# Cache moves due earlier, and the a/b projection as fp32 products on four column groups

## The chip, the cores and the metric

The kernel runs on one core of one Trainium2 chip, in one launch. The metric is the device time of one execution in microseconds (us), as the median of a few runs. Lower is better.

## The reference, cut to what matters

One decoder step is computed for a prompt of 512 tokens and for 8 samples of 4 tokens each (32 tokens), 544 tokens in all, width 1024. Everything is fp32.

```python
shift, scale, gate = jnp.split(jax.nn.silu(c) @ w_cond + b_cond, 3, axis=-1)
h = x * (1 + scale[:, None]) + shift[:, None]
qa, ka, va, za, qkv_b, zb, a_b, b_b, g_a, g_b = split_columns(h @ w_in)   # 11280 columns
# branch A: sliding-window attention, three groups of heads; the samples' keys are
#           cache rows (128, 512 and 2048 of them) followed by their four new rows
# branch B: gated delta rule; its decay comes from a_b and its beta from b_b (8 columns each)
merged = sigmoid(g_a) * (yA @ w_branch_a) + sigmoid(g_b) * (yB @ w_branch_b)
x = LayerNorm(ALPHA * x + gate * (merged @ w_out)) * ln_g + ln_b
# also returned: the samples' caches moved up by four rows, with the new rows at the end
kv_new.append(ext[:, ext.shape[1] - n_buf:])
```

Two pieces of this matter below. The 16 columns a and b of the projection are a small product (1024 by 16) for all 544 tokens. The returned caches are, but for the four new rows, a copy of 84 MB from one place in HBM to another, on which no computation waits.

## The kernel before

**How it is built.** The function `body` doesn't issue instructions. It records them (class `Recorder`), and `Recorder.schedule` then puts them in order with a list scheduler: it keeps its own estimate of when each engine and each operand is free, and takes on each engine the ready operation of lowest rank, then of lowest number. An operation may carry a due time `at`, ahead of which it isn't taken. `emit` then issues everything in that order on five in-order queues (PE, DVE, ACT, POOL, SP); since it is one line of code, all instructions in the profile carry the line L735, and they are told apart by their tiles' names.

**The front.** The scale comes from `cond_block(1, c, m, ...)`, which multiplies silu(c) (`cs`) by a piece `wc` of the conditioning weights: eight fp32 products into four column groups of one bank (`tile_position=(0, 32 * q)`), then `Y`, then products with `sel`, which add the four groups up. Each chunk of `sc` makes `x1`, the scaled x as two parts `x1h` and `x1l` (high part and remainder in float32r). The first three tiles of the projection are built from `x1` while the scale still arrives. Behind them stands the product for a and b: the weight columns 384 to 399 of `W3` are split into high and low part in one tile of 32 columns, `hl`, and for each half of the tokens (272 columns) 16 products `pg<-x1h,hl` and `pg<-x1l,hl` add up in one bank; ACT copies both halves to `abT`. The shift is put on later (`W3` by `sh`, then additions on `ab`), and `gates()` makes the decays from `abT` with products against `sel16` and `selab`, which add the high and low rows.

**The stream.** The rest of the projection, the two branch products and the gates run as a stream of jobs (`stream`): a job's weights are loaded into `wt` (three buffers, 512 KB each), split by ACT into `hi` and by DVE into `lo`, and multiplied with `hhi` and `hlo` (the two parts of h) in 48 products of 272 columns into `pp`. The stream has rank 9, so attention (`pg`), delta rule (`pd`, `pb`) and everything else go ahead of it when they are ready, and it fills the rest. The samples' attention comes in two halves: the first (`slab` tiles) runs beside the prompt's attention, the second (`kv` tiles, 32 loads of 512 KB of keys and values) from about 660 us on, after the samples' delta rule (`S0` tiles).

**The cache moves.** 168 moves of 128 rows each copy the caches from `cache{g}` to `kv{g}_s`, all issued on SP. They have rank 30, the last of all, and are spread evenly by their due times between two numbers:

```python
MOVES = (48.0, 850.0)
    d.at = MOVES[0] + (MOVES[1] - MOVES[0]) * i / len(moves)
```

The scheduler also holds a rank-30 move back while more than four of its eight tracked transfers are in flight. Weight loads, the samples' keys and values, and many small round trips through HBM use the same SP queue.

Of the kernel before, what the change touches and what calls it, by code (L numbers as in the profile page):

```python
# [11 lines left out]
F32 = mybir.dt.float32  # L12
F32R = mybir.dt.float32r
AF = mybir.ActivationFunctionType
# [6 lines left out]
KT = 8  # L21
SEQ = 512
# [3 lines left out]
NT = SEQ + NS  # L26
HF = NT // 2
# [8 lines left out]
BIG = 1e30  # L36
BANKS = (2, 2, 3, 1)
MOVE = 128
MOVES = (48.0, 850.0)
GATES = (110.0, 200.0)  # L40
EARLY_A, EARLY_B = 7, 4
S0B = 7
# [208 lines left out]
class Recorder:  # L251
# [22 lines left out]
    def pool(self, make, name, bufs, side):  # L274
        return Pool(self, make, name, bufs, side)
# [512 lines left out]
def body(ctx, tc, io):  # L788
    rec = Recorder()
    pe, ve, se, ge, sp = rec.engines()  # L790
# [19 lines left out]
    def pg():  # L810
        return psg.tile([128, 512], F32, name="pg", tag="g")
# [4 lines left out]
    def pb_():  # L816
        return psb.tile([128, 512], F32, name="pb", tag="b")
# [14 lines left out]
    def C(name, where="early"):  # L832
        a, n = CCOLS[name]
        return tables[where][:, a:a + n]
# [13 lines left out]
    op = pool(octx, "opool", 9, "right")  # L848
# [41 lines left out]
    xT = fx.tile([128, KT, NT], F32, name="xT")  # L890
    W3 = fx.tile([128, KT, 400], F32, name="W3")
    sc = fx.tile([128, KT, 9], F32, name="sc")
    sh = fx.tile([128, KT, 32], F32, name="sh")
    early_ = op.tile([128, NT], F32, name="cg", tag="o")
    n = CONST[2].shape[1]
# [1 line left out]
    dta = early_[:, n:n + 68].rearrange("p (a b) -> p a b", b=34)  # L897
    shifts = early_[:, n + 68:n + 104].rearrange("p (a b) -> p a b", b=9)
    first = [op.tile([128, NT], F32, name="raw", tag="o") for _ in range(3)]
    abT = op.tile([128, NT], F32, name="abT", tag="o")[0:32]  # L900
    xs = xT[:, :, SEQ:].rearrange("p k (b t) -> p k b t", t=4)
    per_token = lambda t, k, n: t[:, k:k + n, 1:9, None].to_broadcast([128, n, 8, 4])
    cols_of = lambda n: slice(n * HF, (n + 1) * HF)
    with ExitStack() as fctx:
        fr = pool(fctx, "front", 1)
# [27 lines left out]
        sp.dma_start(bnw, io["b_norm_w"])  # L933
        ve.memset(cs, 0.0)
        ge.memset(sh, 0.0)
        th = fr.tile([128, KT, 9], F32, name="th")
        se.activation(th, cT, AF.Tanh, scale=0.5)
        ve.tensor_scalar(th, th, 0.5, 0.5, op0=OP.mult, op1=OP.add)
# [2 lines left out]
        def cond_block(part, at, m, other):  # L941

            ps, wc, w = pb_() if other else pg(), pieces[part, at], 128 * m
            idle = IDLE if (part, at) == (1, 0) else (0, 0, 0)
            rec.rank = -1

            def turn_over(n):
                for _ in range(n):
                    pe.matmul(ps[:, 384:512], ones, ones, start=True, stop=True)

            turn_over(idle[0])
            with rec.together():
                for k in range(KT):
                    q = k % 4
                    pe.matmul(ps[32 * q:32 * q + 32, 0:w].rearrange("p (a b) -> p a b", b=128), cs[:, k, :], wc[:, :, k, :],
                              start=(k < 4), stop=(k >= 4), tile_position=(0, 32 * q)).at = 9.9 * ((part, at) == (1, 1))
                turn_over(idle[1])
            Y = fr.tile([128, 256], F32, name="Y", bufs=2)
            ve.tensor_copy(Y[:, 0:w], ps[:, 0:w])
            pv = ps[:, 256:256 + 16 * m].rearrange("p (a b) -> p a b", b=16)  # L960
            with rec.together():
                for i in range(m):
                    pe.matmul(pv[:, i, 0:9], Y[:, 128 * i:128 * i + 128], C("selc", "first"), start=True, stop=True)
                turn_over(idle[2])
            rec.rank = 0
            return pv[:, :, 0:9], bT[:, 8 * part + at:8 * part + at + m, None].to_broadcast([128, m, 9])

        x1 = [fr.tile([128, KT, NT], F32R, name=f"x1{u}") for u in "hl"]
        sums = [[f()[:, :HF] for _ in range(2)] for f in (pp, pd, pg)]
        for b, (c, m) in enumerate(CHUNKS):  # L970
            pv, bias = cond_block(1, c, m, b % 2)
            kk = slice(c, c + m)
            ve.scalar_tensor_tensor(sc[:, kk], pv, 1.0, bias, op0=OP.add, op1=OP.add)
            for k in range(c, c + m):
                se.activation(x1[0][:, k, :SEQ], xT[:, k, :SEQ], AF.Copy, scale=sc[:, k, 0:1])
                if k == c:
                    ve.tensor_mul(xs[:, kk], xs[:, kk], per_token(sc, c, m))
                    se.activation(x1[0][:, kk, SEQ:], xT[:, kk, SEQ:], AF.Copy)
                    ve.tensor_sub(x1[1][:, kk, SEQ:], xT[:, kk, SEQ:], x1[0][:, kk, SEQ:].bitcast(F32))
                ve.scalar_tensor_tensor(x1[1][:, k, :SEQ], xT[:, k, :SEQ], sc[:, k, 0:1], x1[0][:, k, :SEQ].bitcast(F32),  # L980
                                        op0=OP.mult, op1=OP.subtract)
            hi, lo = (wsp.tile([128, D], F32R, name=n, tag=n)[:, 0:384 * m].rearrange("p (k c) -> p k c", k=m) for n in ("hi", "lo"))
            se.activation(hi, W3[:, kk, 0:384], AF.Copy)
            ve.tensor_sub(lo, W3[:, kk, 0:384], hi.bitcast(F32))
            for k in range(c, c + m):
                for t in range(3):
                    w, w_ = (x[:, k - c, 128 * t:128 * t + 128] for x in (hi, lo))
                    for n in range(2):
                        for a, x in ((w, 0), (w, 1), (w_, 0)):
                            pe.matmul(sums[t][n], a, x1[x][:, k, cols_of(n)], start=(k == 0 and a is w and x == 0),  # L990
                                      stop=(k == KT - 1 and a is w_))
        for t in range(3):
            for n in range(2):
                rec.either(first[t][:, cols_of(n)], sums[t][n])
        hl = fr.tile([128, KT, 32], F32R, name="hl")
        se.activation(hl[:, :, 0:16], W3[:, :, 384:400], AF.Copy)
        ve.tensor_sub(hl[:, :, 16:32], W3[:, :, 384:400], hl[:, :, 0:16].bitcast(F32))
        ps = [pg(), pg()]
        for n in range(2):
            for k in range(KT):  # L1000
                for x in range(2):
                    pe.matmul(ps[n][0:32, :HF], hl[:, k], x1[x][:, k, cols_of(n)],
                              start=(k == 0 and x == 0), stop=(k == KT - 1 and x == 1))
        for n in range(2):
            se.activation(abT[:, cols_of(n)], ps[n][0:32, :HF], AF.Copy)
        for c, m in two_by_two:
            pv, bias = cond_block(0, c, m, c % 4)
            kk = slice(c, c + m)
# [2 lines left out]
        ps, pv = pg(), pb_()  # L1011
        with rec.together():
            for k in range(KT):
                q = k % 4
                pe.matmul(ps[32 * q:32 * q + 32, 0:400], sh[:, k, :], W3[:, k, :], start=(k < 4), stop=(k >= 4),
                          tile_position=(0, 32 * q))
# [80 lines left out]
    for i, (g, b, r0, r1) in enumerate(moves):  # L1097
        d = mv.dma_start(io[f"kv{g}_s"][b, r0:r1], io[f"cache{g}"][b, r0 + 4:r1 + 4])
        d.at = MOVES[0] + (MOVES[1] - MOVES[0]) * i / len(moves)
    rec.rank = 0  # L1100
# [29 lines left out]
    def gates():  # L1130
# [14 lines left out]

        pa = pg()
        for c in range(4):
            pe.matmul(pa[:, c * 16:c * 16 + 16], abT[:, c * 128:(c + 1) * 128], C("sel16", "g")[0:32], start=True, stop=True)
        sab = C("selab", "g").rearrange("p (a b) -> p a b", b=4)
        for h4 in range(4):  # L1150
            pe.matmul(pa[32 * h4:32 * h4 + 32, 64:68], abT[:, SEQ:], sab[0:32, h4, :], start=True, stop=True)
        zero = op.tile([128, NT], F32, name="zero", tag="o")[0:16, 0:512]
        ge.memset(zero, 0.0)
        ab = d1.tile([128, 2, 34], F32, name="ab")
# [36 lines left out]
        g = d1.tile([128, 34], F32, name="g")  # L1191
# [355 lines left out]
    pairs = [{} for _ in range(4)]  # L1547
# [637 lines left out]
    rules = threads.add(chain(delta_rule), 0)  # L2185
    blocks = threads.add(chain(delta_blocks), 1)
    threads.add(gates(), -2)
    threads.add(stream(57 + 4 + EARLY_B), 9)
    ap = pool(actx, "ap", 1)
# [125 lines left out]
    for k in range(0, KT, 2):  # L2315
        name = ("hi", "lo")[k // 4]
# [69 lines left out]
    for tt, n in ((0, 0), (1, 0), (2, 0), (None, 0), (0, 1), (1, 1), (2, 1), (3, 0), (3, 1)):  # L2386
# [3 lines left out]
        q = r[tt]  # L2390
        step = 256 if n and tt == 3 else 512
        for c in range(512 * n, 512 * n + 512, step):
            po = product_out(tt, c, c + step)
            w = slice(c, c + step)
# [129 lines left out]
```

## Time and profile before

| | us |
|---|---|
| median of 3 runs | 878.49 |
| lowest and highest | 874.96, 881.58 |
| the profiled execution: its time | 876.41 |
| its span, first to last instruction | 874.6 |
| mean granted TensorE clock | 0.995 |

| engine | busy us | share of the span |
|---|---|---|
| PE (TensorE) | 860.4 | 98% |
| DVE (VectorE) | 644.2 | 74% |
| ACT (ScalarE) | 452.0 | 52% |
| POOL (GpSimd) | 66.1 | 8% |

[...] The DMA engines are busy for four fifths of the span, moving 236 MB.

### The profile page before, as it was taken

The page shows a single profiled execution, that of the slowest core. Times are in us where ns is not written, and L with a number is a line of the kernel's source. Part 1 is how long each engine was busy: PE and PEld are TensorE (multiplying, and loading weights), DVE is VectorE, ACT ScalarE, POOL GpSimd, SP SyncE. Part 2 cuts the span into 40 slices and gives each one's busy share as a digit, 9 for nine tenths or more (in the row PEclk, how much of TensorE's full clock was granted, in tenths as well). Part 3 has the DMA queues.
Part 4 walks back from the last instruction along what each step waited for, and adds up shares of the span by engine and source line. Part 5 has one row for each costly group of instructions (what it writes and reads, how often), then busy time and mean ns, then how long its engine had stood idle before and what let it go on. Part 6 is the DMA issues. An engine that isn't in the chain of part 4 may idle for free.

```text
span 874.6 us, 20691 instructions
## 1 busy us (share of the span) xinstructions
PE 860.4 (98%) x8152; PEld 812.8 (93%) x8152; DVE 644.2 (74%) x1326; ACT 452.0 (52%) x1071; POOL 66.1 (8%) x167
## 2 busy tenths in 40 slices
PE   8999999999999999999999999999999999999996
PEld 7889999898999999998999998999999999999875
DVE  4775557565447999866999963564999999968547
ACT  3546556765646776446776446733442213334442
POOL 0120110110001010001110000011010000001000
PEclk9999999999999999999999999999999999999998
DMA  9876768756596969979788887469869899989983
GB/s 338 344 217 189 240 216 261 252 203 222 182 265 222 314 213 270 297 218 340 248 270 272 273 254 257 161 215 337 335 186 360 320 354 369 384 284 331 363 289 138
DMA packets 120493, 236.18 MB, mean 270 GB/s; under 512 B 49110, under 2 KB 76576, under 8 KB 117708
## 3 DMA queue, kind: packets, MB, share of 16 engines
q1 hardware_dynamic: 120396, 234.86, 79.6%
q8 instruction: 64, 1.05, 0.5%
q14 instruction: 33, 0.27, 0.1%
HBM read 218.53 MB, written 103.97 MB: 369 GB/s over the span
## 4 chain that ended last, share of the span: by engine, by line
PE 92%; DVE 3%; ACT 2%; DMA 1%; issue 1%; SPq 1%; DVEq 0%
PE pp L735 69%; PE pg L735 10%; PE pd L735 9%; PE pb L735 4%; DMA wc<-in_w_cb 1%; ACT L735 1%; SPq L735 1%; DVE acc L735 0%; DVE lo L735 0%; ACT sq L735 0%; DMA out_kv_s<-in_cache 0%; DVE gt L735 0%; DVE r L735 0%; DVE slab L735 0%; DVE zt L735 0%
## 5 line engine op out<-in xcount | busy, mean ns | idle before, releaser
L735 PE MATMUL pp<-hhi,hi 128*128 128x272 f32 x1360 | 399.1, 293 | 0.5 <-DVE zt L735 0.5
L735 PE MATMUL pp<-hhi,lo 128*128 128x272 f32 x1360 | 397.1, 292 | 0.0
L735 PE MATMUL pp<-hlo,hi 128*128 128x272 f32 x1360 | 395.8, 291 | 0.0
L735 PEld LDWEIGHTS pp<-hhi,hi 128*128 128x128 f32 x1360 | 257.0, 189 | 3.3 <-issue 2.6
L735 PEld LDWEIGHTS pp<-hhi,lo 128*128 128x128 f32 x1360 | 257.0, 189 | 1.8 <-issue 1.1
L735 PEld LDWEIGHTS pp<-hlo,hi 128*128 128x128 f32 x1360 | 257.0, 189 | 1.5 <-issue 0.4
L735 ACT ACTIVATE hi<-wt 128x1024 fp32r<-128x1024 f32 (+1 forms) x101 | 103.4, 1024 | 159.4 <-PE pp L735 134.2
L735 DVE TENSOR_TENSOR lo<-wt,hi 128x1024 fp32r<-128x1024 f32 (+1 forms) x101 | 119.1, 1179 | 84.4 <-ACT hi L735 80.8
L735 DVE SCALAR_TENSOR_TENSOR acc<-ext,cw,acc 128x568 f32<-128x568 f32 x72 | 57.9, 804 | 2.1 <-ACT acc L735 1.1
L735 DVE TENSOR_REDUCE slab<-slab 128x8 f32<-128x512 f32 (+2 forms) x66 | 42.4, 660 | 2.6 <-ACT slab L735 2.5
L735 DVE TENSOR_TENSOR slab<-slab 128x512 f32<-128x512 f32 (+1 forms) x66 | 43.0, 670 | 0.4 <-DMA slab<-in_ks 0.3
L735 ACT ACTIVATE zt<-pp 128x272 f32<-128x272 f32 x48 | 18.7, 390 | 46.1 <-PE pp L735 45.9
L735 ACT ACT_TABLE_LOAD x32 | 41.1, 1283 | 2.4 <-PE pp L735 1.0
L735 PE MATMUL pp<-ybh,lo 128*128 128x272 f32 x128 | 37.1, 290 | 0.0
L735 PE MATMUL pp<-ybh,hi 128*128 128x272 f32 x128 | 36.9, 288 | 0.0
L735 PE MATMUL pp<-ybl,hi 128*128 128x272 f32 x128 | 36.9, 288 | 0.0
L735 ACT ACTIVATE P<-P,st 128x256 f32<-128x256 f32 (+1 forms) x64 | 31.1, 487 | 6.8 <-DVE st L735 6.6
L735 DVE CUSTOM_DVE_ANT_0 P<-pg,bias 128x256 f32<-128x256 f32 (+1 forms) x64 | 23.3, 404 | 12.9 <-PE pg L735 12.9
L735 POOL COPY cx<-ext 128x3 f32<-128x3 f32 (+1 forms) x48 | 22.2, 490 | 140.1 <-ACT ext L735 138.6
L735 ACT ACTIVATE spare<-pp 128x272 f32<-128x272 f32 (+1 forms) x32 | 16.2, 507 | 19.1 <-PE pp L735 19.1
L735 PEld LDWEIGHTS pp<-ybh,lo 128*128 128x128 f32 x128 | 24.2, 189 | 0.6 <-issue 0.4
L735 PEld LDWEIGHTS pp<-ybh,hi 128*128 128x128 f32 x128 | 24.2, 189 | 0.1
(419 smaller groups left out, 1539.0 us busy)
## 6 DMA issues: line engine op xcount, KB each, us to landing
out_kv_s<-in_cache SPq DMA_DIRECT2D x144, 512.0 KB
wt<-in_w_in SPq DMA_DIRECT2D x85, 512.0 KB
out_kv_s<-in_cache SPq DMA_DIRECT2D x24, 496.0 KB
wc<-in_w_cb SPq DMA_DIRECT2D x16, 512.0 KB
slab<-in_ks SPq DMA_DIRECT2D x32, 256.0 KB
slab<-in_vs SPq DMA_DIRECT2D x32, 256.0 KB
kv<-in_ks SPq DMA_DIRECT2D x16, 512.0 KB
kv<-in_vs SPq DMA_DIRECT2D x16, 512.0 KB
```

Of the source, the lines that this page charges most:

```text
L735: getattr(real[x.engine], x.name)(*map(arg, x.args), **{k: arg(v) for k, v in x.kw.items()})
```

## The change

The moves' due times end at 690 instead of 850. The a/b product is taken apart. For the prompt's 512 tokens the scale goes into the weights (`wsc` is `wab` times `sc`, one multiplication on DVE), and the product reads the raw `xT` in fp32: eight products of 512 columns, two into each of four column groups. For the 32 sample tokens, 16 fp32 products of 32 columns go into four column groups. The tile `abT` is now 128 partitions high and holds four partial sums, and the products in `gates()` contract over all 128 partitions, which adds them up. Some lines of the diff:

```diff
-MOVES = (48.0, 850.0)
+MOVES = (48.0, 690.0)
-    abT = op.tile([128, NT], F32, name="abT", tag="o")[0:32]
+    abT = op.tile([128, NT], F32, name="abT", tag="o")
+        wab, wsc = (fr.tile([128, KT, 32], F32, name=name) for name in ("wab", "wsc"))
+        ge.memset(wab, 0.0)
...
+        se.activation(wab[:, :, 0:16], W3[:, :, 384:400], AF.Copy)
+        ve.tensor_mul(wsc, wab, sc[:, :, 0:1].to_broadcast([128, KT, 32]))
+
+        def ab_product(out, pairs):
+            with rec.together():
+                for i, (w, x) in enumerate(pairs):
+                    q = 32 * (i % 4)
+                    pe.matmul(out[q:q + 32], w, x, start=(i < 4), stop=(i >= len(pairs) - 4), tile_position=(0, q))
+
+        ps = pg()
+        rec.rank = -1
+        ab_product(ps, [(wsc[:, k], xT[:, k, :SEQ]) for k in range(KT)])
+        se.activation(abT[:, :SEQ], ps, AF.Copy)
+        rec.rank = 0
...
-        hl = fr.tile([128, KT, 32], F32R, name="hl")
-        se.activation(hl[:, :, 0:16], W3[:, :, 384:400], AF.Copy)
-        ve.tensor_sub(hl[:, :, 16:32], W3[:, :, 384:400], hl[:, :, 0:16].bitcast(F32))
-        ps = [pg(), pg()]
-        for n in range(2):
-            for k in range(KT):
-                for x in range(2):
-                    pe.matmul(ps[n][0:32, :HF], hl[:, k], x1[x][:, k, cols_of(n)],
-                              start=(k == 0 and x == 0), stop=(k == KT - 1 and x == 1))
-        for n in range(2):
-            se.activation(abT[:, cols_of(n)], ps[n][0:32, :HF], AF.Copy)
+        ps = pg()[:, 0:32]
+        ab_product(ps, [(wab[:, k], x1[x][:, k, SEQ:].bitcast(F32)) for k in range(KT) for x in range(2)])
+        se.activation(abT[:, SEQ:], ps, AF.Copy)
```

Because the scheduler decides the order, the change reaches further than these lines: on PE and DVE the order of many instructions after the front differs. Three places show what moves.

On PE, in the front, the prompt's a/b product is put into the stretch where the last chunk of the scale is used (`x1h`, `x1l` by `hi`, `lo`). `wc,cs` is a conditioning product, `sel,Y` the sum of its groups. A piece of the difference, the lines with + being the change:

```order
 L735 MATMUL pp<-x1h,hi 128x272 x2
 L735 MATMUL pd<-x1h,hi 128x272
-L735 MATMUL pg<-wc,cs 32x256 x8
+L735 MATMUL pg<-xT,wsc 32x512 x8
 L735 MATMUL pp<-x1l,hi 128x272
 L735 MATMUL pp<-x1h,lo 128x272
```

The eight products of 512 columns stand where the first conditioning product of the shift stood; that one moves behind the next few products of the stream and there meets the second one, so that two column-group products follow each other directly.

On PE, some 40 rows later, the old a/b product stood between the first products of the stream (`hhi`, `hlo`); in the change the samples' product stands directly behind a conditioning product. First a piece of the difference, then the same place in the change:

```order
 L735 MATMUL pp<-hhi,hi 128x272
 L735 MATMUL pp<-hlo,hi 128x272
-L735 MATMUL pp<-hhi,lo 128x272
-L735 MATMUL pg<-x1h,hl 32x272
-L735 MATMUL pg<-x1l,hl 32x272
```

```order
L735 MATMUL pp<-hhi,hi 128x272
L735 MATMUL pp<-hlo,hi 128x272
L735 MATMUL pb<-wc,cs 32x256 x8
L735 MATMUL pg<-x1h,wab 32x32
L735 MATMUL pg<-x1l,wab 32x32
```

The 32 products of the old form (the first two of which are shown) are gone, and 16 short ones (again two shown) take their place.

On SP, near the end of the program, where the last weights of branch A (`wt<-in_w_ga`) and the output weights (`wo`) are loaded, the order before still holds moves (`out_kv2_s<-in_cache2`) between the loads:

```order
L735 DMA wt_10852<-in_w_in 128x1024
L735 DMA out_kv2_s<-in_cache2 16x8192 x2
L735 DMA wt_10894<-in_w_ga 128x512
L735 DMA out_kv2_s<-in_cache2 16x8192
L735 DMA wo_10935<-in_w_out 128x2x512
```

In the change the same loads follow one another:

```order
L735 DMA wt_10821<-in_w_ga 128x512
L735 DMA wt_10861<-in_w_in 128x1024
L735 DMA wt_10901<-in_w_ga 128x512
L735 DMA wo_10941<-in_w_out 128x2x512
L735 DMA wo_10986<-in_w_out 128x2x512
```

All 168 moves now stand ahead of the first of branch A's weights. Counted along the whole SP order, 126 moves stand ahead of the 81st of the 101 weight tiles before, and 157 do so in the change.

More of the change, by code (lines that the diff above doesn't have):

```diff
@@ L1147, in gates @@
         for c in range(4):
-            pe.matmul(pa[:, c * 16:c * 16 + 16], abT[:, c * 128:(c + 1) * 128], C("sel16", "g")[0:32], start=True, stop=True)
+            pe.matmul(pa[:, c * 16:c * 16 + 16], abT[:, c * 128:(c + 1) * 128], C("sel16", "g"), start=True, stop=True)
         sab = C("selab", "g").rearrange("p (a b) -> p a b", b=4)
         for h4 in range(4):
-            pe.matmul(pa[32 * h4:32 * h4 + 32, 64:68], abT[:, SEQ:], sab[0:32, h4, :], start=True, stop=True)
+            pe.matmul(pa[32 * h4:32 * h4 + 32, 64:68], abT[:, SEQ:], sab[:, h4, :], start=True, stop=True)
         zero = op.tile([128, NT], F32, name="zero", tag="o")[0:16, 0:512]
```

## The prediction

> **What bounds the kernel now.** The page comes first: span, busy time, DMA, and the groups that could matter.
>
> ```profile
> span 874.6 us, 20691 instructions
> PE 860.4 (98%) x8152; PEld 812.8 (93%) x8152; DVE 644.2 (74%) x1326; ACT 452.0 (52%) x1071; POOL 66.1 (8%) x167
> q1 hardware_dynamic: 120396, 234.86, 79.6%
> L735 ACT ACT_TABLE_LOAD x32 | 41.1, 1283 | 2.4 <-PE pp L735 1.0
> out_kv_s<-in_cache SPq DMA_DIRECT2D x144, 512.0 KB
> ```
>
> PE is idle for 874.6 - 860.4 = 14.2 us in all. Whatever another engine or a transfer gains can shorten the kernel only inside these 14.2 us; the rest is PE work, and falls only if PE has less to do. The second view cuts the span where something changes: the front, the stream, a stretch at 405, the time from 690 on (where the moves would be gone), and the end. Columns: length, then PE, PEld, DVE, ACT and POOL busy (and count), granted clock, DMA share, GB/s.
>
> ```profile
> 0.00:5.00 5.00, 3.78 (x16) 3.51 (x17) 0.89 (x6) 1.55 (x2) 0.52 (x5) 1.00 0.55 158
> 5.00:50.00 45.00, 43.30 (x413) 35.17 (x414) 27.52 (x69) 19.79 (x39) 7.14 (x13) 1.00 0.96 346
> 50.00:405.00 355.00, 354.31 (x3551) 337.97 (x3553) 247.53 (x605) 219.32 (x561) 33.03 (x98) 1.00 0.76 240
> 405.00:413.00 8.00, 6.54 (x101) 6.04 (x94) 3.35 (x13) 5.90 (x15) 0.25 (x2) 0.79 0.92 318
> 413.00:690.00 277.00, 276.60 (x2728) 265.96 (x2727) 220.43 (x443) 143.38 (x352) 20.29 (x42) 1.00 0.79 266
> 690.00:850.00 160.00, 158.97 (x1260) 149.59 (x1259) 126.54 (x161) 55.25 (x88) 4.91 (x8) 1.00 0.93 343
> 850.00:866.90 16.90, 16.86 (x99) 14.57 (x97) 13.63 (x26) 6.49 (x15) 0.00 (x0) 1.00 0.56 194
> 866.90:874.70 7.80, 0.00 (x0) 0.00 (x0) 4.31 (x8) 0.29 (x1) 0.00 (x0) 0.67 0.18 67
> ```
>
> The idle time lies in the first 50 us (2.9), in the stretch at 405 (1.5), after 690 (1.0) and behind the last product (7.8, a chain of DVE work and the last store). From 50 to 405 it is 0.7 us out of 355. The third view says what PE waited for; a column is the total, the times and the longest.
>
> ```profile
> PE pg L735 <- issue: 1.5, 1, 1.5
> PE pp L735 <- DVE zt L735: 1.0, 2, 0.5
> PE pg L735 <- DMA wc<-in_w_cb: 0.8, 2, 0.6
> PE pb L735 <- DMA wc<-in_w_cb: 0.7, 1, 0.7
> ```
>
> The only transfers PE waits for are the conditioning weights `wc` of the front, 1.5 us, and those are issued ahead of every move. The 1.0 us behind 690 is a wait for DVE's `zt`.
>
> **The change, part one: the moves.** Would a stream job feel a transfer? The view of the tile `wt` tells when weights are requested and when ACT takes them.
>
> ```profile
> L735 ACT ACTIVATE hi<-wt x101: 629/1058/1077, 36.1 to 807.6; 128x1024 fp32r<-128x1024 f32 x93, 128x512 fp32r<-128x512 f32 x8
> L735 SPq DMA_DIRECT2D wt<-in_w_in x85: 327/337/3009, 25.7 to 797.5; - x85
> L735 SPq DMA_DIRECT2D wt<-in_w_ga x8: 333/334/357, 763.9 to 800.5; - x8
>   PE pp L735: 134.2, 62
> ```
>
> The first tile is asked for at 25.7 and taken at 36.1, the last at 800.5 and 807.6: 7 to 10 us ahead. What ACT waits for ahead of `hi` is PE, 134.2 us over 62 times (PE gives the buffer back); no transfer of `wt` stands there. So weights land with time in hand, and moves may shift them by a few us for nothing. Behind 690 the moves' leaving lowers a DMA share of 0.93, but there PE is already busy for 158.97 of 160 us, and its idle 1.0 us is DVE's. Gain there: between 0 and 1.0 us; I take 0, since the only releaser named is DVE.
>
> Ahead of 690 the load rises. Counted in SP's order, 157 instead of 126 moves stand ahead of the 81st weight tile: 31 more. At the rate of the row 690:850, 343 GB/s, a move of 512 KB takes 1.5 us of all DMA engines, so 31 take 47 us. Free DMA time there, from the shares: 355 x 0.24 + 8 x 0.08 + 277 x 0.21 = 144 us. The load fits into a third of what is free. Each move is issued by SP in its turn, and the same 168 are issued either way. Cost: 0 where transfers have such a margin; the upper bound is the rival below.
>
> **Part two: the a/b product.** What is removed is 32 products of 272 columns. Here are the first and last of ten in a row, in the order of time (start, length), and a column-group product just ahead of them:
>
> ```profile
> 44.97 1.55 PE L735 MATMUL pg<-W,sh 128*32 128x400 f32 x16
> 46.45 0.31 PE L735 MATMUL pg<-x1l,hl 128*32 128x272 f32 x1
> 46.61 0.28 PE L735 MATMUL pg<-x1h,hl 128*32 128x272 f32 x1
> 47.72 0.29 PE L735 MATMUL pg<-x1l,hl 128*32 128x272 f32 x1
> ```
>
> From 46.61 to 47.72 are nine steps: 0.123 us each, so 32 x 0.123 = **3.9 us removed**. These products had only 32 output columns, and cost as much as those with 128.
>
> The prompt's new product: eight fp32 products of 512 columns on four groups. The same form with other widths is there, with 400 columns above (44.97 to the next start at 46.45, 1.48 us) and with 256 here, between two products of the stream's form:
>
> ```profile
> 32.81 0.29 PE L735 MATMUL pg<-x1h,hi 128*128 128x272 f32 x1
> 33.03 1.07 PE L735 MATMUL pb<-wc,cs 128*32 128x256 f32 x16
> 34.03 0.40 PE L735 MATMUL pg<-x1l,hi 128*128 128x272 f32 x1
> 34.26 0.29 PE L735 MATMUL pg<-x1h,lo 128*128 128x272 f32 x1
> ```
>
> 256 columns take 1.00 us, 400 take 1.48: 3.3 ns a column, so 512 take 1.48 + 112 x 0.0033 = 1.85 us. The turn to the other form costs something on both sides: 0.22 instead of 0.12 us ahead of it, 0.23 instead of 0.12 behind. Together 1.85 + 0.2 = **2.05 us added**.
>
> The samples' product: 16 fp32 products of 32 columns, 32 records. The nearest rows are the samples' scores:
>
> ```profile
> 718.55 0.64 PE L735 MATMUL pg<-ks,Qz 128*32 128x32 f32 x48
> 719.12 0.39 PE L735 MATMUL pp<-hlo,hi 128*128 128x272 f32 x1
> ```
>
> 48 records in 0.57 us make 0.38 us for 32. It follows a conditioning product of the same form, so it pays no turn of its own: **0.4 us added**. The lower bound is 0.3 (0.1 us of turn taken off the 0.57), the upper 1.9: in the stretch at 405 the same scores have the 1.5 us pause among them.
>
> The trace's 12 ns for a record decides here. [...]
>
> Two conditioning products that stood alone now follow each other, which saves one turn (0.2 us); the shift's product with `W3` now stands between stream products, which costs 0.1. I leave both out. On DVE, `wsc` (256 elements) replaces a subtraction of 128, on POOL one memset of 256 comes first: both engines idle in that stretch (DVE 27.5 of 45 us, POOL 7.1). The new product's wait for `wsc` stands behind products of the last chunk that wait for ACT's `x1h` from the same scale; if `wsc` were later than these by its own length, PE would wait some 0.3 us, and the whole stream behind it. Between 0 and 0.3; I take 0. ACT gets 38 instead of 32 table loads in the new order, 6 x 1.28 = 7.7 us on an engine that is idle for 422 us.
>
> **The sum.** -3.9 + 2.05 + 0.4 = -1.5 us of PE work, and PE is the bound around it. The span goes from 874.6 to 873.1 and the profiled execution from 876.4 to 874.9. The median of the runs shown is 878.5, 2.1 us above that execution. I put the forecast between 874.9 and 878.5 - 1.5 = 877.0, at **876 us**.
>
> **Rivals.**
>
> *Faster (870 us).* The relief behind 690 counts after all (1.0 us), and the pause at 405 doesn't come again: 1.46 us of waiting for nothing that the profile shows, and a granted clock of 0.79 over 8 us, which is 1.7 us lost. 874.9 - 1.0 - 1.5 - 1.7 = 870.7. For it: nothing in the program asks for the pause. Against: the same group of products stands in the change. Even this is within 1% of 878.5, and no idle time is left to take beyond it but the start and the last 7.8 us, which are untouched.
>
> *Slower (888 us).* The denser moves turn into waits ahead of 690. The place is any in-order engine that stands behind a short chain through HBM: the delta rule's `dblk`, `Ls`, `dtz`, `Tc` and the weights `wv` for the merge of the groups. Two more moves ahead of such a load put 3 us on it; the view of `wv` shows DVE waiting 0.3 us for it already, so it has no margin there. It decides once a load lands later than the work that the schedule has put ahead of its user, about the length of a stream job, 48 x 0.123 = 5.9 us. If four such places lose 3 us each, 874.9 + 12 = 887, and with the median's offset 888. Against: there is twice as much free DMA time as is left to fill, and SP holds a move back while transfers are in flight. [...]
>
> ```profile
> DVE ya L735 <- DMA wv<-dw: 0.3, 1, 0.3
> ```
>
> *The a/b part gives nothing (878 us).* The new products' bank or `wsc` comes late by as much as is saved: a rival with the sign of no change.
>
> **How the numbers follow.** Forecast 0.70, no gain 0.15, faster 0.08, slower 0.07. About 1% is what a measurement of this kernel tells from no change: 878.5 less 1% is 869.7, plus 1% is 887.3. The first two and most of the faster case lie within. The range leaves out the far end of the slower case and takes in the scatter of the runs before (875 to 881.6): 869 to 884. Faster by over 1%: 0.06; within 1%: 0.88; slower: 0.06.
>
> **What the next profile would show.** Right: PE idle still near 14 us; between 5 and 50 us the stream begins 1.5 us earlier; `pg<-xT,wsc` takes 1.85 us to the next start, `x1h,wab` and `x1l,wab` together 0.4; the DMA share behind 690 falls below 0.93 and rises above 0.79 ahead of it, with PE's busy time as before. Wrong: a PE wait for `Tc`, `wt`, `S0` or `ya` of more than 2 us in the list of waits, a second stretch with a clock below 1.00, or PE idle of over 20 us.

## The result, and the profile after

The changed kernel takes **884.78 us** (median of 17 runs, 878.57 to 890.03); the kernel before took 877.45 us beside it (17 runs, 874.58 to 881.58). The ratio is **1.0086, 95% interval 1.0069 to 1.0104**: 0.9% slower, 7.5 us, where the prediction's sum had 1.5 us of gain. The profiled execution of the changed kernel took 890.03 us, 5 us above its median, so its pauses are longer than usual; a second one stands under the experiments.

The page first: span, engines, and the queue that brings PE's instructions.

```profile
span 888.2 us, 20709 instructions
...
PE 864.4 (97%) x8168; PEld 815.8 (92%) x8168; DVE 643.9 (72%) x1329; ACT 457.4 (51%) x1074; POOL 68.5 (8%) x168
...
q8 instruction: 64, 1.05, 0.5%
```

PE is idle for 23.8 us (888.2 - 864.4), not 14.2. The windows, cut as in the prediction and with the same columns:

```profile
5.00:50.00 45.00, 43.14 (x439) 34.37 (x440) 26.81 (x62) 20.00 (x39) 7.96 (x12) 1.00 0.98 350
50.00:405.00 355.00, 349.95 (x3445) 333.16 (x3444) 244.04 (x600) 213.56 (x547) 33.73 (x96) 0.99 0.78 252
405.00:413.00 8.00, 5.31 (x67) 5.00 (x66) 0.69 (x3) 2.54 (x7) 0.34 (x2) 0.63 0.56 205
413.00:690.00 277.00, 273.42 (x2745) 262.53 (x2745) 215.16 (x450) 153.70 (x369) 20.41 (x44) 0.99 0.88 297
690.00:850.00 160.00, 159.00 (x1290) 152.59 (x1293) 134.77 (x167) 55.16 (x88) 5.32 (x8) 1.00 0.76 274
```

The moves did what the change says: behind 690 the DMA share is 0.76 where it was 0.93, and from 413 to 690 it is 0.88 where it was 0.79. PE's idle time grew ahead of 690 alone: 5.1 instead of 0.7 us from 50 to 405, 2.7 instead of 1.5 at 405, 3.6 instead of 0.4 from 413 to 690; behind 690 it is 1.0 as before. The list of PE's waits names what ended them (total, times, longest):

```profile
PE pg L735 <- issue: 4.0, 1, 4.0
PE pd L735 <- issue: 3.5, 2, 2.1
PE pp L735 <- ACT ext L735: 1.4, 1, 1.4
PE pd L735 <- ACT S L735: 1.3, 1, 1.3
```

"issue" is a wait for nothing that the profile shows; I call these three the pauses. The timeline has two of them in the middle of a run of short products of one kind, with nothing between them:

```profile
163.02 0.55 PE L735 MATMUL pd<-W,Xc 32*32 32x16 f32 x43
165.67 0.51 PE L735 MATMUL pd<-W,Xc 32*32 32x16 f32 x21 [2.10 <-issue]
...
403.19 0.46 PE L735 MATMUL pg<-ks,Qz 128*32 128x32 f32 x29
407.69 0.53 PE L735 MATMUL pg<-ks,Qz 128*32 128x32 f32 x19 [4.04 <-issue]
```

With each the granted clock is halved. Windows cut to these stretches; the clock is the third number from the end:

```profile
164.80:175.10 10.30, 9.43 (x84) 7.04 (x84) 3.56 (x13) 3.42 (x11) 0.78 (x2) 0.50 0.62 218
407.00:414.00 7.00, 6.31 (x115) 5.93 (x114) 1.44 (x4) 3.41 (x8) 0.34 (x2) 0.51 0.38 139
540.20:543.70 3.50, 3.50 (x61) 3.25 (x59) 0.00 (x0) 0.72 (x3) 0.00 (x0) 0.51 0.94 322
```

That is some 20 us at half speed, 10.2 us lost, where the profile of before has 3.4 us of it (1.7 lost). The pauses grew from 2.0 to 7.5 us (4.0 + 3.5). Pauses and half clock together make 14.0 us, about the 13.6 us between the two profiles.

**What the pauses are.** PE's stream has 8168 weight loads, 8168 products and 166 waits and drains, 16502 instructions; queue q8 brought 64 packets, 1.05 MB, so 16 KB each and, since 64 x 256 = 16384, some 256 instructions each. I call such a packet a block and its transfer the fetch. Numbered in the order of their start, all three pauses stand at an instruction whose number leaves 193 when it is divided by 256. In the traces of both kernels packet m of q8 starts after instruction 256m + 128, by 4.6 us on average in the kernel before and 4.8 in the changed one, and takes 1.0 us; PE never starts instruction 256m + 449 sooner than 1.2 us behind the packet's end. Together these are 6.8 us on average (the expectations below count with 6.7), and in that time PE has 321 instructions to go on with (449 - 128, some 160 products with their loads). They take PE 19 us in the median, and where they take 12 us or more the fetch doesn't show: PE's step into instruction 256m + 449 is 0.23 us at most. Among the short products of the delta rule and the samples' scores they take 4 to 7 us, and there the block can come late. I call these the short blocks.

**What stands ahead of them.** SP's timeline shows four moves of some 512 KB in one go just ahead of the fetches of the first two (which start at 163.5 and 405.3). Ahead of the third (536.5) it shows one move at 529.64 and three of the four from 534.17 on; the last of these goes out at 536.97, behind the start of the fetch.

```profile
157.85 2.41 SPq L735 DMA_DIRECT2D out_kv_s<-in_cache  x4
...
398.70 3.64 SPq L735 DMA_DIRECT2D out_kv_s<-in_cache  x4
...
529.64 1.86 SPq L735 DMA_DIRECT2D out_kv_s<-in_cache  x1
...
534.17 3.30 SPq L735 DMA_DIRECT2D out_kv_s<-in_cache  x4
```

### The profile page after: what moved, and what is told of

It reads as the page before. It is cut to its first block, busy times and chain, and to the rows that moved or that the text cites. A ratio compares the mean times of both kernels' runs of the same rounds, so it can differ in the third digit from the quotient of the medians.

```text
span 888.2 us, 20709 instructions
## 1 busy us (share of the span) xinstructions
PE 864.4 (97%) x8168; PEld 815.8 (92%) x8168; DVE 643.9 (72%) x1329; ACT 457.4 (51%) x1074; POOL 68.5 (8%) x168
## 3 DMA queue, kind: packets, MB, share of 16 engines
q8 instruction: 64, 1.05, 0.5%
## 4 chain that ended last, share of the span: by engine, by line
PE 88%; ACT 4%; DMA 3%; DVE 3%; issue 2%; SPq 0%; POOL 0%; DVEq 0%; ACTq 0%
PE pp L735 67%; PE pg L735 9%; PE pd L735 8%; PE pb L735 4%; DMA W<-in_w 2%; ACT L735 1%; ACT hi L735 1%; DMA rbo<-dO 1%; DVE r L735 1%; ACT sq L735 1%; SPq L735 0%; DVE lo L735 0%; ACT ext L735 0%; DVE zt L735 0%; ACT acc L735 0%
## 5 line engine op out<-in xcount | busy, mean ns | idle before, releaser
L735 PEld LDWEIGHTS pp<-ybl,hi 128*128 128x128 f32 x128 | 24.1, 189 | 0.1
```

What stands on the lines that cost most here:

```text
L735: getattr(real[x.engine], x.name)(*map(arg, x.args), **{k: arg(v) for k, v in x.kw.items()})
```

## The experiments

All ratios are to the kernel before, run beside them on the same chip. The expectations speak of four theories. A, position: the change moved the ends of the blocks to places where the products are short. B, density: with more moves ahead of 690 every transfer is later. C, late blocks: moves that go out just ahead of a short block delay its fetch. D, order: the planner's new order of the work costs time by itself.

**One part alone.** The first kernel has the a/b part with the old due time, the second the new due time with the old a/b product; each is ordered anew by the planner.

```diff
 (changed kernel)                 (kernel before)
-MOVES = (48.0, 690.0)           -MOVES = (48.0, 850.0)
+MOVES = (48.0, 850.0)           +MOVES = (48.0, 690.0)
```

> The a/b part alone: the changed kernel with the moves due until 850 again. Theories: A (position): PE reads its instructions in blocks of 256 (16 KB, a packet each), and where the end of a block falls among short products PE pauses until the next block is in; the change moved these ends to worse places. B (density): the denser moves before 690 make every transfer later, that of the instruction blocks and those of the data. Counted from the order of this kernel, with the durations of the products in the two traces, 5 block ends leave less than the 6.7 us that a block seems to need, short by 14.9 us together (the kernel before 6 and 13.8, the changed one 7 and 19.4). A: near the kernel before, 876 to 879 us, and one or two pauses without a releaser. B: 877.5 - 1.5 = 876 us, PE idle near 14 us. Both theories allow a time below 880; a time of 883 or more would say that the loss sits in the a/b part itself.

> The moves alone: the kernel before with the moves due until 690, so that its order and its transfers change and its a/b product doesn't. By the same count 5 block ends are short, by 12.2 us together, a little less than in the kernel before (13.8). A (position): 876 to 878.5 us, no slower than the kernel before. B (density): as much slower as the changed kernel was against its own sum, 877.5 + 8.8 = 886 us, with the same waits without a releaser at other places. In between (880 to 883): both count.

Measured: the a/b part alone 876.3 us, ratio 0.9991 (0.9972 to 1.001); the moves alone 879.66 us, 1.0028 (1.0007 to 1.0049). Neither makes the 0.9%, and the sum of both, 1.0019, doesn't either. Position alone doesn't decide (the second should have been no slower), and neither does density (it should have reached 886). The second kernel's profile has one pause of 1.8 us, at 163, and 3.4 us of half clock behind it.

**The blocks moved by half their length.** The changed kernel in its own order with narrow products in the place of three idle ones at the start:

```diff
+if turn in (6, 7, 8):            # PE's sixth to eighth product: idle ones
+    ps, w, m = map(arg, x.args)
+    for i in range(35 if turn == 6 else 0):
+        q = 32 * (i % 4)
+        nc.tensor.matmul(ps[q:q + 32, 0:32], w[:, 0:32], m[:, 0:32], start=True, stop=True, tile_position=(0, q))
+    continue
```

> The changed kernel in its own order, with every instruction from 4 us on standing 128 places later in PE's stream: three of the eight idle products at the start are replaced by 35 narrow ones on four column groups (140 instructions instead of 12). The block ends move by half a block, and nothing else does. The count of what they are short falls from 19.4 to 9.8 us; the end that stood among the products pg<-ks,Qz at 407, with the pause of 4.0 us, is gone. A (position): 874 to 880 us, PE idle below 18 us, no pause at pg<-ks,Qz. B (density): no change, 884 to 885 us, the pauses only at other places. That the 35 products cost something is bounded by 64 more records of 12 to 24 ns, 0.8 to 1.5 us, less the three idle products of 0.45 us: about nothing.

Measured: 885.39 us, 1.0093 (1.0067 to 1.0119), no gain. The waits for "issue" in its profile:

```profile
PE pd L745 <- issue: 6.8, 4, 3.6
...
PE pp L745 <- issue: 1.9, 1, 1.9
```

The pause at `pg<-ks,Qz` is gone, as the count said, and others stand at the block ends that the count names (167, 399, 404, 530, 536). The count finds the places. It doesn't give the size: at 536 PE stood for 3.6 us at the end of a stretch whose 321 instructions take 6.9 us in the kernels where nothing stops them, since the fetch started 9.1 us after instruction 256m + 128 (in the changed kernel 4.8 us on average). When the fetch starts decides, not only where the block ends.

**The moves' data taken out.** First the changed kernel, later the kernel before. Each move copies 8 of its 128 rows and leaves the rest of the copy out:

```diff
 d.at = MOVES[0] + (MOVES[1] - MOVES[0]) * i / len(moves)
+d.args = (io[f"kv{g}_s"][b, r0:r0 + 8], io[f"cache{g}"][b, r0 + 4:r0 + 12])
```

> The changed kernel in its own order with 8 of each move's 128 rows copied: the issues stay in their places, the rest of the cache copy is left out. The DMA share before 690 should fall below 0.5. B (density): the blocks and the data come in time, the pauses go, and the time is that of PE's work: 888.2 - 7.5 (pauses) - 10.2 (half clock) = 871 in the profile's span, 870 to 874 us. A (position): blocks are fetched faster on free queues, but the ends stand where they stood, so that some pauses stay; 874 to 880 us with PE still pausing at pg<-ks,Qz near 405. If the time stays at 884, neither transfers nor their density have a part in it.

> The kernel before in its order with 8 of each move's 128 rows copied, the rest of the cache copy left out: the counterpart of the changed kernel with 8 rows, which took 0.9972 of the time before. The two differ only in the order and the a/b product, with no load to speak of. By the sum of the prediction (-1.5 us of PE work) this one takes 1.5 us more than its counterpart, 0.9989, 876 us; that the changed order costs time of its own (theory D) would put it at or below 0.9972.

Measured: changed 875.05 us, 0.9972 (0.9957 to 0.9987); before 873.61 us, 0.9960 (0.9944 to 0.9975). The fetches start after 3.7 and 3.6 us on average. (The DMA engines are not free even so: their share from 50 to 690 is 0.54 in the changed kernel's case, where it was 0.82.) So the moves' data costs the changed kernel 0.0114, 10.0 us, and the kernel before 0.0040, 3.5 us: 6.5 of the 7.5 us lie here. What is left without the data has the wrong sign as well: the changed kernel should be 1.5 us faster and is 1 us slower, if anything (the intervals overlap). The waits of the two, changed first, then before:

```profile
PE pp L735 <- ACT ext L735: 1.4, 1, 1.4
PE pd L735 <- ACT S L735: 1.3, 1, 1.3
PE pd L735 <- ACT XF L735: 1.1, 1, 1.1
```

```profile
PE pg L735 <- DVE ones L735: 1.1, 1, 1.1
PE pp L735 <- DVE zt L735: 1.0, 2, 0.5
PE pd L735 <- issue: 0.6, 1, 0.6
```

In this pair the clock is halved nowhere ahead of the last product, so PE's busy time on their pages can be compared: 856.1 us in the changed kernel and 858.6 in the kernel before. The a/b part does save work, 2.5 us of it. But PE's idle time is 17.6 us against 12.6: the new order has 3.8 us of waits for ACT that the old hasn't. For `S` the timeline of ACT (changed kernel, 8 rows) shows why:

```profile
434.51 1.28 ACT L735 ACT_TABLE_LOAD   x1
435.81 0.51 ACT L735 ACTIVATE P<-P,st 128x256 f32<-128x256 f32 x1
...
436.31 0.26 ACT L735 ACTIVATE S<-pd 128x128 f32<-128x128 f32 x1
```

A table load of 1.28 us stands ahead of the copy of `S` out of its bank, and PE waits 1.3 us. Theory D has a part, but a small one.

**The moves put back, or forward, without the planner.** Engines' own work in its order, moves put among SP's issues by their due time alone:

```diff
+SPREAD = (850.0 - MOVES[0]) / (MOVES[1] - MOVES[0])    # the second kernel: 690.0
...
+for kind, x in self.order:       # moves taken out of the order, put in again by due time
+    if kind == "op" and not getattr(x, "move", False):
+        while moves and MOVES[0] + (moves[0].at - MOVES[0]) * SPREAD < x.start:
+            order.append(("op", moves.pop(0)))
...
```

> The changed kernel with every engine's own work in its order, and only the 168 moves put back among SP's other issues to where they are due until 850 us. What is known by now: the a/b part alone and the moves alone cost little, the 128 places took nothing away, and with most of the moves' data left out the loss was gone. Theory C (late blocks): a move's packets delay the fetch of PE's next instruction block, and PE pauses where this falls on a block that is short; what decides is how many moves go out just ahead of such a block. Then spreading the moves takes away most of the loss: 876 to 880 us, at most 4 us of pauses without a releaser. Theory D (order): the order of the work itself loses the 8 us, the moves' place has no part in it: 883 to 886 us.

> The counterpart: the kernel before with every engine's own work in its order, and only the moves put forward among SP's issues to where they are due until 690 us. Theory C (late blocks): pauses without a releaser where moves now go out ahead of a short block, 879 to 886 us. Theory D (order): as before, 876 to 878.5 us.

Measured: 907.45 us, 1.0333 (1.0309 to 1.0357), and 893.88 us, 1.0182 (1.0157 to 1.0208). Both lie above what either theory allowed, so neither kernel tests them. They show what I had left out: the planner holds a move back while transfers are in flight, and here nothing does. Loads are late. In the first kernel DVE waits 9.9 us for `wv`, a load that the prediction's slower rival had named, and PE's longest wait stands behind that one:

```profile
DVE ya L744 <- DMA wv<-dw: 9.9, 1, 9.9
...
PE pp L744 <- DVE spare L744: 9.7, 1, 9.7
PE pd L744 <- DVE mv L744: 4.5, 1, 4.5
```

The first kernel's "issue" pauses are still 4.9 us together. Neither kernel says anything on density.

**The twelve moves ahead of the pauses, and twelve others.** Both kernels copy 8 rows instead of 128 in twelve moves and leave the rest of these out. The numbers count the moves in the order of their issue:

```diff
+if i in (27, 28, 29, 30, 77, 78, 79, 80, 109, 110, 111, 112):   # the control: 90 to 101
+    d.args = (io[f"kv{g}_s"][b, r0:r0 + 8], io[f"cache{g}"][b, r0 + 4:r0 + 12])
```

> The changed kernel in its order, with 8 of 128 rows copied by the twelve moves that its trace shows going out in the few us ahead of its three pauses (four at 157.9 to 159.7, four at 398.7 to 401.8, four from 529 to 535); the rest of these twelve pieces is left out, the other 156 moves are whole. Theory C (late blocks): the three blocks come in time; the pauses of 4.0, 2.1 and 1.4 us go, and the half clock behind them (10.2 us in the profile): of the loss of 7.5 us in the median 4 to 7 go, 878 to 881 us. If the blocks are late for any other reason (the weights' transfers, PE's own fetch): no change, 884 to 885 us.

> The control for that: the same twelve moves' worth of data left out, but of the twelve moves that go out between 440 and 480 us, where no block is short. Theory C (late blocks): no change, 883 to 886 us, the three pauses as they were. If it is the total of bytes that counts (a mean load): as much gained as with the twelve ahead of the pauses.

Measured: without the twelve ahead of the pauses **876.06 us, 0.9986** (0.9971 to 1.0001); without twelve others 882.68 us, 1.0066 (1.0041 to 1.0091). Much the same bytes are worth 8.8 us at the one place and 1.8 us at the other, where the interval reaches the changed kernel's own. In the control's profile the pause among the scores stands (3.3 us), the one at 163 is short, and at 537 PE doesn't stop; that execution took 880.70 us, 2 us less than the control's median:

```profile
PE pg L735 <- issue: 3.3, 1, 3.3
PE pd L735 <- issue: 1.0, 2, 0.6
```

From the records of the packets and products, in us (the last column is PE's step across the block's end, 0.01 where it doesn't stop):

| short block, PE there at | changed: fetch starts after | start to start at its end | twelve out: fetch starts after | start to start |
|---|---|---|---|---|
| 163 | 6.6 | 2.28 | 4.0 | 0.01 |
| 403 | 5.9 | 4.23 | 1.6 | under 0.01 |
| 537 | 4.5 | 1.56 | 1.7 | under 0.01 |

The scores that had the pause of 4.04 us run through, and the clock stays up (timeline and windows without the twelve):

```profile
398.53 0.66 PE L735 MATMUL pg<-ks,Qz 128*32 128x32 f32 x48
```

```profile
164.80:175.10 10.30, 10.30 (x162) 8.80 (x160) 5.67 (x17) 8.18 (x21) 1.79 (x4) 1.00 0.71 235
398.00:405.00 7.00, 7.00 (x182) 6.31 (x174) 4.67 (x11) 4.84 (x12) 1.12 (x4) 1.00 0.50 153
```

This settles where the loss is: moves ahead of three short blocks, the late blocks, and the half clock behind them. That the moves must come in a burst, and not only stand there, no run shows by itself.

**The same execution again.**

> The changed kernel as it is, profiled once more. If the pauses come from the place of the block ends and of the moves, which are the same in every execution, the same two or three stand there again (at 163 to 167, 403 to 407, 537) with other lengths; if they come and go by chance, others do. 878 to 890 us.

883.47 us. Two pauses stand at the same places with other lengths: 1.0 us at 164 and 2.8 us at 402, the second with 3.4 us of half clock behind it, the only half clock ahead of the last product. At 537 PE stops for 0.2 us alone, and a pause of 1.1 us stands at 284, at the end of another short block. So the places are given by the order, and which of them bite changes. In its list of waits:

```profile
PE pg L735 <- issue: 2.8, 1, 2.8
PE pd L735 <- issue: 2.3, 3, 1.1
```

**The twelve moves put behind the dense work, whole.** Also in the kernel before, for eight moves ahead of its two pauses:

```diff
+# HOLD: moves 27-30: 157, 77-80: 405, 109-112: 540 (before: 43-46: 265, 67-70: 399)
+to = HOLD.get(getattr(x, "move", None)) if sp else None
...
+    held.setdefault(to, []).append((kind, x))
...
+order += held.pop(n, [])         # behind SP's issue number n
```

> The changed kernel complete, every move copied whole, with the twelve moves ahead of its three pauses put behind the dense work in SP's order: four from 158 to behind the issues at 172, four from 399 to behind the weight tile at 414, four from 530 to 535 behind the weight tile at 551. Theory C (a burst of moves just ahead of a short block delays that block): the pauses and the half clock at these places go without a byte less, 876 to 878 us, 1.0 us or more of it the a/b part's gain against the kernel before. If it was only the bytes left out that helped before: 882 to 885 us. A rival on the other side: SP, which issues in order, holds up a weight tile or a slab behind the bunched moves; then a wait for a DMA of over 2 us appears and the time stays above 880.

> The same done to the kernel before: the four moves at 396 to 399 and the four at 276 to 278, ahead of its pauses of 1.5 and 0.5 us, go behind the next slabs. Theory C: 1.5 + 0.5 + 1.7 (half clock) = up to 3.7 us in the profile, 874 to 876.5 us in the median. If its pauses have another cause: 877 us.

Measured: 882.35 us, 1.0059 (1.004 to 1.0078), and 879.33 us, 1.0025 (1.0003 to 1.0048). In the first the three pauses are gone, and the named rival came: bunched elsewhere, the moves hold up other data.

```profile
PE pd L748 <- DVE S L748: 2.9, 1, 2.9
PE pp L748 <- DVE spare L748: 2.1, 1, 2.1
```

DVE comes late with `S` because an operation ahead of it waits for values of the samples' attention:

```profile
426.10 1.34 DVE L748 TENSOR_TENSOR slab<-slab 128x512 f32<-128x512 f32 x2 [3.20 <-DMA slab<-in_vs]
427.36 0.34 DVE L748 SCALAR_TENSOR_TENSOR S<-S,etot,pd 128x128 f32<-128x128 f32 x1
```

Behind this wait the clock is halved again, for 3.4 us. In the second kernel it is the same: no "issue" pause over 0.3 us, but waits for `st` (2.6 us) and `rbo` (2.1 us). So eight moves held by hand gained nothing there.

**Smaller bursts, and other due times.** One number of the planner each:

```diff
-    FEW = 4
+    FEW = 2                      # first with 690, then with 850
-MOVES = (48.0, 690.0)
+MOVES = (48.0, 670.0)            # the third; the fourth: 710.0
```

> The changed kernel with one number of the planner: a move waits until two transfers of SP are in flight, not four (FEW = 2), so that the planner makes no bursts of four moves; due until 690 as in the change. Theory C (bursts ahead of short blocks): 877 to 880 us, fetches of PE's blocks sooner on average (below 4.6 us after their trigger), pauses below 3 us together. If the mean density of the moves decides: as the changed kernel, 883 to 886 us.

> The same with the moves due until 850: the a/b part, no bursts of four, and the old pace. Both theories: 874 to 877 us. It is the version that should beat both kernels: the a/b part's 1.5 us and up to 2 us of the pauses of the kernel before. If moves that wait for two in flight come too late, the copy's end shows behind 860 us and the time is above 878.

> The changed kernel with the moves due until 670 instead of 690: a little denser, another order. Counted from its order, 8 block ends leave less than the 6.7 us, short by 17.6 us together (the changed kernel 7 and 19.4). If density decides: 885 to 887 us. If it is the place of the bursts and of the block ends: anything from 877 to 885 by chance, by the count 881 to 884.

> The changed kernel with the moves due until 710: a little less dense, another order; by the same count 5 block ends are short, by 10.0 us together. If density decides: 882 to 885 us, near the changed kernel's 884.8 since 20 us out of 642 are little. If it is the place of the bursts and of the block ends: 876 to 880 us.

Measured: 954.84 us, 1.0886 (1.0861 to 1.0911); 958.69 us, 1.0939 (1.0914 to 1.0963); 877.31 us, **1.0003** (0.9987 to 1.002); 878.04 us, 1.0017 (1.0001 to 1.0033). With bursts of two the fetches come sooner (4.2 instead of 4.8 us on average) and PE is done at 869 instead of 880 us, but the copy of the caches isn't; the window behind 860 of the first shows DMA at work and PE not:

```profile
860.00:960.00 100.00, 9.48 (x66) 8.51 (x64) 11.07 (x22) 3.19 (x7) 0.00 (x0) 0.56 0.92 304
```

The rival that I had named for 850 struck both. The other two settle the question of density: 670 is denser than the change and loses nothing, 710 is hardly less dense and loses 1.5 us. My count of short blocks gave 670 a time of 881 to 884 us and so was wrong on it. What the change lost is the loss of one order among several, not of a due time of 690.

**Moves kept away by the planner.** No byte left out, no number of the order set by hand:

```diff
+QUIET = ((149.0, 168.0), (266.0, 284.0), (383.0, 397.0), (506.0, 523.0), (594.0, 606.0))
 clear = lanes.setdefault(False, [0.0] * 8)[-self.FEW]
+clear = max([clear] + [end for start, end in QUIET if start <= t < end])
-MOVES = (48.0, 690.0)
+MOVES = (48.0, 770.0)            # in the second of the two
```

> The changed kernel, every move whole and due until 690, with five stretches of the planner's time in which it issues no move: 149 to 168, 266 to 284, 383 to 397, 506 to 523 and 594 to 606, each from 6 us ahead of the fetch of a short instruction block to the block's end. The planner makes its own order around them, so that no transfer stands in another's way. Theory C (a burst of moves ahead of a short block): the pauses without a releaser fall below 2 us together and 876 to 879 us come out at a density that is higher than the change's between the stretches. If density decides: 885 us or more. The rival is that the order that comes out has waits of its own (table loads of ACT, loads behind the bunched moves), then 880 to 883.

> The same five stretches with the moves due until 770, the candidate to beat both kernels: the a/b part's 1.5 us are kept, the pauses of 3 to 4 us that the kernel before still has are gone, against 1 to 3 us of waits that the order makes: 873 to 876.5 us, 0.996 to 0.9995 of the kernel before.

Measured: due until 690, 879.4 us, 1.0019 (1.0001 to 1.0037), 5.9 us better than the change at the same due time, with every byte copied. Its profile has 1.0 us of "issue" in all and no half clock ahead of the last product, but 4.5 us of waits for `ext`, `NTs` and `XF`, from its order. The other one, due until 770, takes **871.72 us, 0.9940** (0.9918 to 0.9963). This one beats both kernels. Its page and the head of its list of waits:

```profile
PE 856.1 (99%) x8168; PEld 808.9 (93%) x8168; DVE 643.3 (74%) x1329; ACT 449.7 (52%) x1068; POOL 73.7 (8%) x168
```

```profile
PE pg L737 <- DVE ones L737: 1.1, 1, 1.1
PE pp L737 <- ACT qs L737: 0.5, 1, 0.5
...
PE pg L737 <- issue: 0.2, 1, 0.2
```

There is no half clock ahead of its last product, and hardly a wait for ACT. How much of its gain is the quiet stretches and how much an order with few waits stays open: no kernel due until 770 without them was run.

## Why the prediction was wrong, point by point

**Part two held.** A product's record is longer than its price: in the prediction's rows from 46.45 to 47.72 a record lasts some 0.3 us and the next one starts 0.12 us later. So prices are read from start to start. The prompt's product takes 1.86 us to the next start (predicted 1.85), the samples' 0.40 us (predicted 0.40):

```profile
30.07 1.93 PE L735 MATMUL pg<-xT,wsc 128*32 128x512 f32 x16
31.93 0.39 PE L735 MATMUL pp<-x1l,hi 128*128 128x272 f32 x1
...
42.72 0.19 PE L735 MATMUL pg<-x1h,wab 128*32 128x32 f32 x1
...
43.12 0.39 PE L735 MATMUL pp<-hhi,lo 128*128 128x272 f32 x1
```

The work that PE saves is 2.5 us in the pair with 8 rows, where the sum had 1.5; where the other 1.0 us comes from wasn't looked into.

**The step that failed is part one's "Cost: 0 where transfers have such a margin".** It failed twice over. The margin was looked up for transfers that appear in the list of waits, the weight tiles and the front's `wc`; PE's own instruction blocks appear there only as "issue", with no name. And the room was counted as a mean, 47 us of load into 144 us that are free, where the moves go out in fours and a short block has 4 to 7 us. Put at 0, the cost was 6.5 us more than the kernel before pays (10.0 against 3.5): late blocks, and the half clock behind them.

**The pause at 405 was read the wrong way round.** The prediction called it a wait for nothing that the profile shows and gave it a part in the faster rival only, as something that might not come again. It was a visible sample of the mechanism: the end of a short block, four moves ahead of it (at 396 to 399 in the kernel before), the half clock behind it. Without the moves' data, and with these four held, it is gone. A pause without a known cause that may go may as well come more often.

**The slower rival had the cause and the wrong victim.** Denser moves did turn into waits ahead of 690, as it said (PE idle there 11.4 us in place of 2.6); it priced four data chains at 3 us each and gave 888 a chance of 0.07. The waits stood at three instruction blocks, and more than half of the profile's loss (8.5 of 13.6 us) was the clock behind them, which it hadn't priced. Density itself, on which the rival rested, wasn't the cause: due until 670 nothing is lost. Two of its figures are off as well: 887 and the median's offset of 2.1 us make 889, not 888, and the free DMA time of 144 us is three times the 47 us of load, not twice.

**ACT's six table loads weren't free.** "7.7 us on an engine that is idle for 422 us" is again a mean: a load of 1.28 us ahead of `S` was on PE's path. The new order's waits for ACT, 3.8 us, are more than the 2.5 us that the a/b part saves.

**Two of the signs of being wrong that the prediction named appeared:** PE idle of over 20 us, and a second stretch with a reduced clock. The third, a wait of over 2 us for the data that it listed, did not.

## What to carry to other kernels

A wait that the profile can't name can be a transfer: count the engine's instructions up to it. Here all such pauses of the changed kernel's profile left the same remainder (193 by 256) and ended 1.3 to 1.5 us behind a packet of q8, and without the data of the twelve moves that went out in the 10 us ahead of them the kernel was 8.8 us faster. Free DMA time is to be read in the stretch where a transfer has to arrive soon (here within 4 to 7 us), not as a mean over hundreds of us. Where a scheduler writes the order, a change of one number gives another draw: run neighbours of the number (here 670, 690, 710: 1.0003, 1.0086, 1.0017) before a gain or a loss is put down to what the change says.

## What the runs showed of the hardware

- PE's instructions arrive as DMA packets on a queue of their own, some 256 to a packet of 16 KB (64 packets, 1.05 MB, for 16502 instructions). In the changed kernel's trace PE steps from one block's end on within 0.23 us at 60 of 63 ends; at the other three, among products that start 9 to 17 ns after one another, PE stood for 1.4, 2.1 and 4.0 us.
- The fetch starts 3.6 to 3.7 us on average after instruction 256m + 128 without the moves' data, 4.6 to 4.8 us with it (the kernel before and the changed one); the longest with it were 9.1 and 11.1 us.
- Pauses of 1.4, 4.0 and 2.1 us among short products came with half clock for 3.4, 6.8 and 10.2 us, from 540.26, 407.14 and 164.79 on: 1.4 us behind the end of the first, 0.6 and 0.9 us ahead of the end of the others. Not every such pause did: the half clock behind 537 came after a pause of 1.4 us, while a pause of 2.3 us at 167, in the kernel with its blocks moved, had none behind it. What decides between these no run shows.
